# Sums of the Winograd products kept in PSUM, and the modulation units divided anew between VectorE and TensorE

## The chip, the cores and the metric

The kernel runs on one core of one Trainium2 chip. The metric is the device time of one execution in microseconds (us). The kernel before took 2699.28 us, the median of three runs (2695.43 to 2701.18).

## The reference, cut to what matters

Two layers are computed on 640 tokens (512 latent, 128 context) of 1024 dimensions. Each layer is a half-step SwiGLU FFN, a mixer of three head groups, and a second FFN half; after each of the three stands a LayerNorm. Each of the three is steered by a shift, a scale and a gate that come from a conditioning vector:

```python
mod = (silu(cond) @ w_mod[l] + b_mod[l]).reshape(9, 1024)      # for the latent and for the context tokens
h = x * (1 + mod[3 * slot + 1]) + mod[3 * slot]
f = (silu(h @ w1) * (h @ w3)) @ w2                             # FFN half, 1024 -> 2816 -> 1024
x = layernorm(alpha * x + 0.5 * mod[3 * slot + 2] * f)
```

All of it is in float32. A product is formed as three passes over operands that are split in a high and a low part (hi x hi, hi x lo, lo x hi).

## The kernel before, in words

**An FFN half.** The 2816 hidden columns are 22 tiles of 128, taken in the chunks 0-4, 4-7, 7-10, 10-14, 14-18 and 18-22. The first three tiles of a half are computed plainly; each of the other 19 is a `Pair`: the two weight tiles (w1 and w3) and the two halves of the tokens (320 columns each, LO and HI) are multiplied as a 2 x 2 block product by Winograd's form of Strassen's scheme, seven block products instead of eight. A block product is 12 matmuls of 320 columns. The chunks after the first hold 3, 3, 4, 4 and 4 pairs. After the pairs of a chunk come its rows: eight output tiles of `w2`, whose results VectorE adds to x (L610). `begun` starts the first two rows without the chunk's last hidden tile.

**Weights.** `Stream` (from L220) loads a pair's two tiles, GpSimd forms the sums s1 to s4 of their blocks (L259, four instructions for each pair), ScalarE rounds each block to its high part (L299, `wh`), and VectorE, or GpSimd for s2 and s4, forms the low part (L306, `wl`). There are six slots of each; a cast is issued five blocks ahead, so that it waits for the product before the one that is being issued to leave its slot.

**A pair, `Pair.run` from L898.** The products come in the order b11, b21, t4, t2, t3, t1, b22; P1 to P7 stand for them below. Each has a PSUM bank of its own (p1, p2, p6, p7, p3, and the two of a double bank p4 and p5). ScalarE copies p1 to SBUF (L895); VectorE forms the sums that Winograd's form wants, seven instructions that each add one bank to a tile in SBUF (L858, called from `c11`, `u2`'s lambda, `u3`, `u4` and `c12`). Then come SiLU of both halves on ScalarE (L863, L877), the gate products on VectorE (`gate1` L865, which calls the helper at L858, and `gate2` L881), the rounding `gh` on ScalarE (L886) and its low part `gl` on VectorE (L891).

**Order.** What follows a product is put in the list `later`, and `slot()` issues it after the next product's matmuls have been issued, so each engine's queue has it one product later; what such a function returns goes to the slot after that. The engines work through their queues in order. `mods(0)`, `mods(1)` and `mods(2)` stand after P2, P4 and P6 of a pair, and one call stands after each row.

**PSUM.** Four single banks (pool `pss`) serve p1, p2, p6, p7, p3 and others; a new tile takes the bank that was given back first.

**Modulation.** There are 144 units (layer, one of nine vectors, one of eight tiles of 128 columns), each 512 KB of `w_mod`. The first 24 are done on TensorE at the start. Of the other 120, some go to VectorE in an FFN half (`vec_mods`, L437: four SCALAR_TENSOR_TENSOR of 128 x 512 for each unit, L460, each with the read of its accumulator, and one small instruction, L463); `mods` issues (4 n + 4) / 95 of them at each call for n units, from the second chunk on. The others go to TensorE in a mixer (`mod_beside`, L411: 8 matmuls at L397 and one for the unit before, at L415). Such a unit is done beside each of the first `len(modq)` of 40 score units of the mixer, and ScalarE takes out the result (L422, L425). Before, 16 units go to VectorE in each of the first three halves, and 40 and 32 to TensorE in the two mixers.

Of the kernel before, what the change touches and what calls it, by code (L numbers as in the profile page):

```python
# [7 lines left out]
F32 = mybir.dt.float32  # L8
F32R = mybir.dt.float32r
BF16 = mybir.dt.bfloat16  # L10
AF = mybir.ActivationFunctionType
ALU = mybir.AluOpType
# [5 lines left out]
KD = D // P  # L18
T = 640
# [11 lines left out]
NC = 3  # L31
HN = T // 2
SLOTS = 6
BLOCKS = ("a11", "a12", "a22", "s2", "s3", "s1", "s4")
NEG = -1.0e30
CONST = (("cond", 16), ("bmod", 144), ("lng", 48), ("lnb", 48), ("sink", 16), ("subg", 2), ("gq", 4), ("sel", 2), 
         ("gkv", 256))
# [68 lines left out]
def trunk_kernel(tc, I, O):  # L106
    nc = tc.nc
    V, S, G, PE = nc.vector, nc.scalar, nc.gpsimd, nc.tensor
    from contextlib import ExitStack
    with ExitStack() as es:  # L110
# [10 lines left out]
        pe_ = pst = pool("e", 21)  # L121
# [6 lines left out]
        pm = pool("wm", 4)  # L128
# [7 lines left out]
        def u(p, n, dt=F32, cols=T, nm="u"):  # L136
            return p.tile([P, cols], dt, tag=nm, name=n)
# [3 lines left out]
        def uid():  # L141
            cnt[0] += 1
            return cnt[0]

        def bank(n="s"):
            return pss.tile([P, 512], F32, tag="s", name=f"{n}{uid()}")

        def dbl(n="d"):
            return psd.tile([P, 2, 512], F32, tag="d", name=f"{n}{uid()}")
# [173 lines left out]
        ws = Stream()  # L323
# [22 lines left out]
        def start(g):  # L346

            next(g)
            tasks.append(g)
# [8 lines left out]
        modq = []  # L358
# [76 lines left out]
        vecq = []  # L435
# [40 lines left out]
        def split(hi, lo, src):  # L476
            S.copy(hi, src)  # L477
            V.tensor_tensor(out=lo, in0=src, in1=hi.bitcast(F32), op=ALU.subtract)  # L478
# [334 lines left out]
        later = []  # L813

        def slot():

            cur, later[:] = later[:], []
            for fn in cur:
                nxt = fn()
                if nxt:  # L820
                    later.append(nxt)
# [8 lines left out]
        class Pair:  # L830


            def __init__(self, h, tb, last):
                self.last = last
                self.b11, self.b21, self.b22 = ([[a[:, c] for a in h[k]] for k in ks]
                                                for ks, c in ((range(4), slice(0, HN)), (range(4, 8), slice(0, HN)),
                                                              (range(4, 8), slice(HN, T))))
                self.t1, self.t2, self.t3, self.t4 = (Quarter(tb, i) for i in range(4))
                self.m, self.sl = u(pe_, f"pm{uid()}"), None

            def out(self):
                self.gh, self.gl = u(pe_, f"gh{uid()}", F32R), u(pe_, f"gl{uid()}", F32R)
                return self.gh, self.gl

            def mms(self, out, w, b, k):
                for i, (a, c) in enumerate(((0, 0), (0, 1), (1, 0))):
                    PE.matmul(out[:, :HN], w[a][:, k, :], b[k][c], start=k == 0 and i == 0, stop=k == 3 and i == 2)  # L847

            def prod(self, out, b, post=None, w=None):
                w = w or ws.get()  # L850
                for k in range(4):
                    self.mms(out, w, b, k)
                slot()
                if post:
                    later.append(post)

            def op(self, o, a, b, f):
                V.tensor_tensor(out=o, in0=a, in1=b[:, :HN], op=f)  # L858

            def c11(self, p2):  # L860
                self.sl = u(pe_, f"sl{uid()}")
                self.op(self.sl[:, LO], self.m[:, LO], p2, ALU.add)
                return lambda: S.activation(self.sl[:, LO], self.sl[:, LO], AF.Silu) and None  # L863

            def gate1(self):  # L865
                self.op(self.g[:, LO], self.g[:, LO], self.sl, ALU.mult)
                return self.half if self.last else None

            def half(self):
                split(self.gh[:, LO], self.gl[:, LO], self.g[:, LO])  # L870

            def c12(self, p3):
                self.op(self.sl[:, HI], self.m[:, LO], p3, ALU.add)
                return self.silu2

            def silu2(self):
                S.activation(self.sl[:, HI], self.sl[:, HI], AF.Silu)  # L877
                return self.gate2

            def gate2(self):  # L880
                V.tensor_tensor(out=self.g[:, HI], in0=self.g[:, HI], in1=self.sl[:, HI], op=ALU.mult)  # L881
                return self.hi

            def hi(self):
                c = HI if self.last else slice(0, T)
                S.copy(self.gh[:, c], self.g[:, c])  # L886
                return self.lo

            def lo(self):
                c = HI if self.last else slice(0, T)  # L890
                V.tensor_tensor(out=self.gl[:, c], in0=self.g[:, c], in1=self.gh[:, c].bitcast(F32), op=ALU.subtract)  # L891

            def start(self):
                p1, p2 = bank("p1"), bank("p2")
                self.prod(p1, self.b11, lambda: S.copy(self.m[:, LO], p1[:, :HN]) and None)  # L895
                self.prod(p2, self.b21, lambda: self.c11(p2))

            def run(self, mods, begun=False):  # L898
                m, op = self.m, self.op
                if not begun:  # L900
                    self.start()
                mods(0)
                p45 = dbl("p4")
                p4, p5 = p45[:, 0, :], p45[:, 1, :]
                self.prod(p4, self.t4)
                p6 = bank("p6")
                self.prod(p6, self.t2, lambda: op(m[:, LO], m[:, LO], p6, ALU.add))
                mods(1)
                p7 = bank("p7")

                def u3():
                    op(m[:, HI], m[:, LO], p7, ALU.add)
                    self.g = u(pe_, f"gf{uid()}")
                    op(self.g[:, LO], m[:, HI], p4, ALU.subtract)
                    return self.gate1
                self.prod(p7, self.t3, u3)

                def u4():
                    op(self.g[:, HI], m[:, HI], p5, ALU.add)
                    op(m[:, LO], m[:, LO], p5, ALU.add)  # L920
                self.prod(p5, self.t1, u4)
                mods(2)
                p3 = bank("p3")
                self.prod(p3, self.b22, lambda: self.c12(p3))

            def run_first(self, mods, other, ts):

                m, op = self.m, self.op
                self.start()
                mods(0)  # L930
                other.start()
                p3 = bank("p3")
                self.prod(p3, self.b22, None, ws.get(4))
                w22 = ws.get(0)
                p45, p6, p7 = dbl("p4"), bank("p6"), bank("p7")
                p4, p5 = p45[:, 0, :], p45[:, 1, :]
                wq = [ws.get(0), ws.get(0), ws.get(2), w22]
                for k in range(4):
                    for o, w, b in zip((p5, p7, p6, p4), wq, (self.t1, self.t3, self.t2, self.t4)):
                        self.mms(o, w, b, k)  # L940
                    mods(k)
                    next(ts, 0)
                slot()

                def post():
                    self.g = u(pe_, f"gf{uid()}")
                    op(m[:, LO], m[:, LO], p6, ALU.add)
                    op(m[:, HI], m[:, LO], p7, ALU.add)
                    op(self.g[:, LO], m[:, HI], p4, ALU.subtract)
                    op(self.g[:, HI], m[:, HI], p5, ALU.add)  # L950
                    op(m[:, LO], m[:, LO], p5, ALU.add)
                    later.append(self.gate1)
                    return self.c12(p3)
                later.append(post)

        LO, HI = slice(0, HN), slice(HN, T)

# [1089 lines left out]
        h = new_h()  # L2047
        first = [dbl("n"), dbl("n"), [bank("n"), bank("n")]]
# [23 lines left out]
        ts = tb_steps(tb, h)  # L2072
# [26 lines left out]
        for l in range(DEPTH):  # L2099
            if l:  # L2100
                tb, ts = tb_next
            h, first = ffn(l, 0, h, first, 0 if l else KD, 2 * KD, lambda a, n, b: rows_norm(a, n, l, 0, (l, 1), b),
                           alpha_first if l == 0 else lambda: alpha_x(l - 1, 2), tb, ts)
            modq += [vecq.pop(0) for _ in range((4 if l else 5) * KD)]
            h, first = mixer(l, h, first, lambda a, n, b: rows_norm(a, n, l, 1, (l, 2), b))
            nxt = (l + 1, 0) if l + 1 < DEPTH else None
            tb, ts = tb_next
            h, first = ffn(l, 1, h, first, 0, 0 if l else 2 * KD, lambda a, n, b: rows_norm(a, n, l, 2, nxt, b),
                           lambda: alpha_x(l, 1), tb, ts)


# [88 lines left out]
```

## Time and profile before

| what | value |
|---|---|
| median of three runs | 2699.28 us |
| the profiled execution | 2705.26 us, its span 2703.3 us |
| mean granted clock of TensorE | 0.976 |
| busy: TensorE, VectorE, ScalarE, GpSimd | 95%, 77%, 43%, 46% |

Times in the profile are microseconds from the start of the span. PE is TensorE, PEld its weight load, DVE VectorE, ACT ScalarE, POOL GpSimd, SP the queue that issues DMAs. A row `out<-in` names the tiles; L858 is line 858 of the kernel. PEclk is the clock that TensorE was granted, as a share of 2.4 GHz. Records of matmuls overlap, so that their mean duration is longer than the time from one to the next.

### The profile page before, as it was taken

What the parts mean: (1) busy time and instruction counts of PE and PEld (TensorE: products, weight loads), DVE (VectorE), ACT (ScalarE), POOL (GpSimd) and SP (SyncE); (2) the same over time, 40 slices, a digit from 0 to 9 for tenths busy, and PEclk for the clock granted to TensorE, in tenths of its full rate; (3) what the DMA queues carried; (4) which work ended last, traced back from release to release, by engine and by line L of the source; (5) the groups of instructions that cost most, each with busy time, mean ns of one, the idle gap of its engine ahead of it and who ended that gap; (6) DMA issues with size and microseconds to landing.
All of it is one profiled execution on the core that took longest, in us unless ns stands there. A gap on an engine that the chain in (4) does not pass through costs nothing. (4 is left out here: it accounts for less than half of the span.)

```text
span 2703.3 us, 49877 instructions
## 1 busy us (share of the span) xinstructions
PE 2555.0 (95%) x18662; PEld 2453.0 (91%) x18662; DVE 2072.3 (77%) x3759; ACT 1175.9 (43%) x2596; POOL 1244.0 (46%) x973
## 2 busy tenths in 40 slices
PE   7999999899999999999989999998998999999997
PEld 6999999888778999999989999998887798999997
DVE  6599889856764879988987998898476558777776
ACT  5233333545575533333353333334545745334333
POOL 2345445522444554544555454454233456435545
PEclk9999999999999999999989999998999999999998
DMA  7333332354344223333222333323543331222222
GB/s 273 116 98 101 111 97 83 117 152 136 91 130 156 71 96 100 103 101 109 68 83 84 112 103 101 110 87 108 158 134 98 103 114 40 82 82 87 79 86 71
DMA packets 130545, 285.89 MB, mean 106 GB/s; under 512 B 16832, under 2 KB 34560, under 8 KB 129664
## 3 DMA queue, kind: packets, MB, share of 16 engines
q1 hardware_dynamic: 130304, 282.70, 33.2%
q8 instruction: 148, 2.42, 0.4%
q14 instruction: 93, 0.76, 0.1%
HBM read 254.95 MB, written 8.81 MB: 98 GB/s over the span
## 5 line engine op out<-in xcount | busy, mean ns | idle before, releaser
L306 DVE TENSOR_TENSOR wl<-wr,wh 128x512 fp32r<-128x512 f32 (+1 forms) x524 | 518.3, 1003 | 74.1 <-ACT wh L299 72.5
L299 ACT CAST wh<-wr 128x512 fp32r<-128x512 f32 (+1 forms) x570 | 333.3, 607 | 479.4 <-DMA wr<-in_w 296.9
L485 PE MATMUL o<-gh,wh 128*128 128x256 f32 (+1 forms) x1408 | 439.5, 312 | 19.4 <-ACT gh L886 11.7
L485 PE MATMUL o<-gl,wh 128*128 128x256 f32 (+1 forms) x1408 | 439.0, 312 | 1.8 <-DVE gl L478 0.3
L485 PE MATMUL o<-gh,wl 128*128 128x256 f32 (+1 forms) x1408 | 436.7, 310 | 0.0
L847 PE MATMUL p<-hh,wh 128*128 128x320 f32 x1216 | 378.4, 311 | 16.8 <-DVE pm L858 16.8
L847 PE MATMUL p<-hl,wh 128*128 128x320 f32 x1216 | 378.2, 311 | 6.2 <-DVE hl L1010 6.2
L847 PE MATMUL p<-hh,wl 128*128 128x320 f32 x1216 | 378.1, 311 | 0.0
L259 POOL TENSOR_TENSOR ws<-wr 128x512 f32<-128x512 f32 x76 | 111.5, 1468 | 545.8 <-DMA wr<-in_w 482.8
L299 ACT CAST wh<-ws 128x512 fp32r<-128x512 f32 x304 | 185.9, 621 | 361.6 <-PE p L847 153.4
L306 POOL TENSOR_TENSOR wl<-ws,wh 128x512 fp32r<-128x512 f32 x152 | 241.3, 1591 | 193.6 <-ACT wh L299 193.1
L610 DVE SCALAR_TENSOR_TENSOR x<-o,gat,x 128x128 f32<-128x128 f32 (+2 forms) x404 | 192.9, 524 | 139.6 <-PE o L485 136.6
L485 PEld LDWEIGHTS o<-gh,wh 128*128 128x128 f32 x1408 | 267.8, 190 | 23.0 <-ACT gh L886 14.5
L485 PEld LDWEIGHTS o<-gl,wh 128*128 128x128 f32 x1408 | 268.1, 190 | 6.7 <-DVE gl L891 4.8
L485 PEld LDWEIGHTS o<-gh,wl 128*128 128x128 f32 x1408 | 267.9, 190 | 0.0
L847 PEld LDWEIGHTS p<-hh,wh 128*128 128x128 f32 x1216 | 229.9, 189 | 19.0 <-issue 18.9
L847 PEld LDWEIGHTS p<-hl,wh 128*128 128x128 f32 x1216 | 230.0, 189 | 7.4 <-DVE hl L1010 7.4
L847 PEld LDWEIGHTS p<-hh,wl 128*128 128x128 f32 x1216 | 230.0, 189 | 0.3 <-DVE wl L306 0.3
L460 DVE SCALAR_TENSOR_TENSOR scr<-wv,cb 128x512 f32<-128x512 f32 x192 | 181.2, 944 | 0.0
L259 POOL TENSOR_TENSOR ws<-wr,wr 128x512 f32<-128x512 f32 x76 | 130.2, 1713 | 0.0
L259 POOL TENSOR_TENSOR ws<-wr,ws 128x512 f32<-128x512 f32 x76 | 129.9, 1709 | 0.0
L259 POOL TENSOR_TENSOR ws<-ws,wr 128x512 f32<-128x512 f32 x76 | 119.1, 1567 | 6.0
(434 smaller groups left out, 6633.9 us busy)
## 6 DMA issues: line engine op xcount, KB each, us to landing
wr<-in_w SPq DMA_DIRECT2D x176, 512.0 KB, 4.2
wm<-in_wmod SPq DMA_DIRECT2D x192, 256.0 KB, 3.9
wr<-in_w SPq DMA_DIRECT2D x128, 256.0 KB, 2.7
wv<-in_wmt SPq DMA_DIRECT2D x96, 256.0 KB, 4.0
wr<-in_w SPq DMA_DIRECT2D x64, 192.0 KB, 2.4
wr<-in_wint SPq DMA_DIRECT2D x24, 512.0 KB, 4.2
wr<-in_wo SPq DMA_DIRECT2D x16, 512.0 KB, 3.8
xd<-x SPq DMA_DIRECT2D x16, 320.0 KB, 5.1
```

The costliest lines, as they stand in the source:

```text
L259: G.tensor_tensor(out=o, in0=x0, in1=x1, op=op)
L299: S.copy(hl[0], src[:, c0:c1])
L306: eng.tensor_tensor(out=t2, in0=src, in1=t.bitcast(F32), op=ALU.subtract)
L460: V.scalar_tensor_tensor(out=scr, in0=w[2 * i + hf], scalar=1.0, in1=cb[:, 2 * st + hf, :], op0=ALU.mult, op1=ALU.mult, accum_out=a[:, 2 * ...
L485: PE.matmul(out[:, :cn], whl[a][:, k, :], b[:, c0:c0 + cn], start=k == 0 and i == 0, stop=k == n - 1 and i == 2)
L610: V.scalar_tensor_tensor(out=c, in0=src, scalar=gat[:, d, s:s + 1], in1=c, op0=ALU.mult, op1=ALU.add)
L847: PE.matmul(out[:, :HN], w[a][:, k, :], b[k][c], start=k == 0 and i == 0, stop=k == 3 and i == 2)
```

## The change: what it does

Within a pair, products that are only added to each other go into one bank: p1, then t2's product, then t3's are accumulated in `px`, and t1's product and b22's in `pz`. Between two of them ScalarE copies the sum so far to SBUF (to `sl` or to `g`). The order of the products becomes b11, b21, t4, t2, t1, t3, b22, and the order of the weight blocks follows it. VectorE keeps four of the seven additions, ScalarE makes four copies instead of one, a pair takes four single banks and no double one, and the two gate products become one of 640 columns but in the last pair of a chunk.

In each of the first three FFN halves VectorE gets 24 units instead of 16, and the mixers get 24 and 24 instead of 40 and 32. `run_first`, which nothing calls, goes.

```diff
-BLOCKS = ("a11", "a12", "a22", "s2", "s3", "s1", "s4")
+BLOCKS = ("a11", "a12", "a22", "s2", "s1", "s3", "s4")
...
-            def prod(self, out, b, post=None, w=None):
-                w = w or ws.get()
+            def prod(self, out, b, post, more=False):
+
+                w = ws.get()
                 for k in range(4):
-                    self.mms(out, w, b, k)
+                    for i, (a, c) in enumerate(((0, 0), (0, 1), (1, 0))):
+                        PE.matmul(out[:, :HN], w[a][:, k, :], b[k][c], start=not more and k == 0 and i == 0, stop=k == 3 and i == 2,
+                                  skip_group_check=more)
                 slot()
-                if post:
-                    later.append(post)
+                later.append(post)
+
+            def add(self, o, ps, f=ALU.add):
+                V.tensor_tensor(out=o, in0=ps[:, :HN], in1=o, op=f)
+
+            def gate(self, c):
+                V.tensor_tensor(out=self.g[:, c], in0=self.g[:, c], in1=self.sl[:, c], op=ALU.mult)
+
+            def split(self, c, nxt=None):
+
                 S.copy(self.gh[:, c], self.g[:, c])
+
+                def lo():
+                    V.tensor_tensor(out=self.gl[:, c], in0=self.g[:, c], in1=self.gh[:, c].bitcast(F32), op=ALU.subtract)
+                    return nxt
+                return lo
+
+            def run(self, mods):
+
+                sl = self.sl = u(pe_, f"sl{uid()}")
+                px, py = bank("px"), bank("py")
+                self.prod(px, self.b11, lambda: S.copy(sl[:, LO], px[:, :HN]) and None)
+
+                def c11():
+                    self.add(sl[:, LO], py)
+                    return lambda: S.activation(sl[:, LO], sl[:, LO], AF.Silu) and None
+                self.prod(py, self.b21, c11)
                 mods(0)
+                pw = bank("pw")
+
+                def c4():
+                    self.g = u(pe_, f"gf{uid()}")
+                    S.copy(self.g[:, LO], pw[:, :HN])
+                self.prod(pw, self.t4, c4)
+                self.prod(px, self.t2, lambda: S.copy(sl[:, HI], px[:, :HN]) and None, True)
                 mods(1)
+                pz = bank("pz")
+                self.prod(pz, self.t1, lambda: S.copy(self.g[:, HI], pz[:, :HN]) and None)
+
+                def c2():
+                    self.add(self.g[:, LO], px, ALU.subtract)
+                    self.add(self.g[:, HI], px)
+                    if self.last:
+                        self.gate(LO)
+                        return lambda: self.split(LO)
+                self.prod(px, self.t3, c2, True)
                 mods(2)
+
+                def c12():
+                    self.add(sl[:, HI], pz)
+                    return silu
+
+                def silu():
+                    S.activation(sl[:, HI], sl[:, HI], AF.Silu)
+                    return gate
+
+                def gate():
+                    c = HI if self.last else slice(0, T)
+                    self.gate(c)
+                    return lambda: self.split(c)
+                self.prod(pz, self.b22, c12, True)
...
-            h, first = ffn(l, 0, h, first, 0 if l else KD, 2 * KD, lambda a, n, b: rows_norm(a, n, l, 0, (l, 1), b),
+            h, first = ffn(l, 0, h, first, 0 if l else KD, 3 * KD, lambda a, n, b: rows_norm(a, n, l, 0, (l, 1), b),
...
-            modq += [vecq.pop(0) for _ in range((4 if l else 5) * KD)]
+            modq += [vecq.pop(0) for _ in range(3 * KD)]
...
-            h, first = ffn(l, 1, h, first, 0, 0 if l else 2 * KD, lambda a, n, b: rows_norm(a, n, l, 2, nxt, b),
+            h, first = ffn(l, 1, h, first, 0, 0 if l else 3 * KD, lambda a, n, b: rows_norm(a, n, l, 2, nxt, b),
```

Of the old code the helpers `op`, `c11`, `gate1`, `half`, `c12`, `silu2`, `gate2`, `hi`, `lo`, `start` and the old `run` go; they stand in the listing above.

## Rows read from the trace of the kernel before

**Rows 1.** The page, part 1: TensorE, busy us and share.
```profile
PE 2555.0 (95%) x18662; PEld 2453.0 (91%) x18662; DVE 2072.3 (77%) x3759; ACT 1175.9 (43%) x2596; POOL 1244.0 (46%) x973
```
**Rows 2.** Windows of the four halves: length, PE, PEld, DVE, ACT, POOL, PEclk, DMA.
```profile
134.14:470.21 336.07, 326.09 (x2187) 323.25 (x2187) 302.88 (x505) 122.78 (x230) 167.93 (x103) 0.99 0.31 98
999.23:1336.72 337.49, 327.12 (x2187) 323.66 (x2187) 305.23 (x508) 123.75 (x231) 167.46 (x103) 0.99 0.31 97
1474.59:1807.68 333.09, 324.71 (x2187) 322.08 (x2187) 303.41 (x505) 123.17 (x230) 165.97 (x103) 0.99 0.31 99
2331.43:2651.66 320.23, 320.23 (x2187) 320.23 (x2187) 240.38 (x373) 125.93 (x232) 156.09 (x103) 1.00 0.26 81
```
**Rows 3.** Windows of chunks of four pairs and of their rows, second and last half.
```profile
1202.45:1254.19 51.74, 49.94 (x339) 49.45 (x339) 49.83 (x74) 21.38 (x40) 30.85 (x19) 1.00 0.29 93
1254.19:1283.56 29.37, 28.48 (x192) 28.02 (x192) 22.58 (x45) 7.30 (x13) 7.75 (x5) 1.00 0.40 129
...
2524.84:2574.28 49.44, 49.44 (x339) 49.44 (x339) 41.92 (x59) 22.79 (x42) 29.61 (x19) 1.00 0.23 70
2574.28:2602.39 28.11, 28.11 (x194) 28.11 (x194) 14.54 (x28) 6.62 (x13) 6.83 (x5) 1.00 0.33 104
```
**Rows 4.** Waits: who waited for whom, us in total, times, longest.
```profile
PE p L847 <- DVE pm L858: 16.8, 8, 3.5
...
PE o L485 <- ACT gh L886: 11.7, 13, 1.1
```
**Rows 5.** Timeline of PE, P2 of a chunk's fourth pair: start, us, what it waited for.
```profile
1243.39 0.39 PE L847 MATMUL p<-hh,wh 128*128 128x320 f32 x1 [1.80 <-DVE pm L858]
```
**Rows 6.** Timeline of DVE, second and third pair of that chunk.
```profile
1222.29 0.47 DVE L858 TENSOR_TENSOR sl<-pm,p 128x320 f32<-128x320 f32 x1
...
1225.71 1.92 DVE L891 TENSOR_TENSOR gl<-gf,gh 128x640 fp32r<-128x640 f32 x1
...
1236.53 1.57 DVE L881 TENSOR_TENSOR gf<-gf,sl 128x320 f32<-128x320 f32 x1
1238.02 0.47 DVE L858 TENSOR_TENSOR sl<-pm,p 128x320 f32<-128x320 f32 x1
```
**Rows 7.** Timeline of DVE, third pair of the last half's chunk.
```profile
2553.65 0.47 DVE L858 TENSOR_TENSOR sl<-pm,p 128x320 f32<-128x320 f32 x1
```
**Rows 8.** Groups by line: busy us, mean ns of one, idle time before.
```profile
L460 DVE SCALAR_TENSOR_TENSOR scr<-wv,cb 128x512 f32<-128x512 f32 x192 | 181.2, 944 | 0.0
...
L895 ACT COPY pm<-p 128x320 f32<-128x320 f32 x76 | 31.2, 410 | 0.0
L460 DVE DVE_READ_ACCUMULATOR scr<-wv,cb 128x1 f32 x192 | 15.2, 79 | 0.0
```
**Rows 9.** Tile scr and line 858: ns shortest/median/longest, first and last start.
```profile
L460 DVE SCALAR_TENSOR_TENSOR scr<-wv,cb x192: 675/683/1830, 131.8 to 1814.7; 128x512 f32<-128x512 f32 x192
...
L858 DVE TENSOR_TENSOR pm<-pm,p x228: 472/475/489, 97.9 to 2651.7; 128x320 f32<-128x320 f32 x114
```
**Rows 10.** Timeline of ACT behind the late sum of the second pair.
```profile
1222.40 0.73 ACT L886 CAST gh<-gf 128x640 fp32r<-128x640 f32 x1 [1.63 <-DVE gf L881]
1223.04 0.46 ACT L863 ACTIVATE sl<-sl 128x320 f32<-128x320 f32 x1
1223.41 0.60 ACT L299 CAST wh<-wr 128x512 fp32r<-128x512 f32 x1
```
**Rows 11.** Window at a lowered clock, just behind a wait of PE.
```profile
1325.20:1328.60 3.40, 3.40 (x15) 3.40 (x14) 3.30 (x10) 0.00 (x0) 0.00 (x0) 0.51 0.30 87
```
**Rows 12.** Timeline of PE, a modulation unit in the first mixer.
```profile
844.44 0.28 PE L415 MATMUL t<-const,ms 128*128 128x2 f32 x2
844.65 0.64 PE L397 MATMUL t<-wm,silc 128*32 128x128 f32 x16
845.23 0.44 PE L1133 MATMUL tr<-idn,ep 128*128 128x128 f32 x2
```
**Rows 13.** Window of the first mixer's last 16 score units.
```profile
789.48:844.33 54.85, 51.93 (x628) 43.49 (x627) 25.31 (x73) 35.41 (x120) 18.36 (x30) 1.00 0.48 150
```

More of the change, by code (lines that the diff above doesn't have):

```diff
@@ L838, in __init__ @@
                 self.t1, self.t2, self.t3, self.t4 = (Quarter(tb, i) for i in range(4))
-                self.m, self.sl = u(pe_, f"pm{uid()}"), None
             def out(self):
@@ L843, in out @@
                 return self.gh, self.gl
-            def mms(self, out, w, b, k):
-                for i, (a, c) in enumerate(((0, 0), (0, 1), (1, 0))):
-                    PE.matmul(out[:, :HN], w[a][:, k, :], b[k][c], start=k == 0 and i == 0, stop=k == 3 and i == 2)
-            def prod(self, out, b, post=None, w=None):
-                w = w or ws.get()
+            def prod(self, out, b, post, more=False):
+                w = ws.get()
                 for k in range(4):
-                    self.mms(out, w, b, k)
+                    for i, (a, c) in enumerate(((0, 0), (0, 1), (1, 0))):
+                        PE.matmul(out[:, :HN], w[a][:, k, :], b[k][c], start=not more and k == 0 and i == 0, stop=k == 3 and i == 2,
+                                  skip_group_check=more)
@@ L853, in prod @@
                 slot()
-                if post:
-                    later.append(post)
[L857 to L882, printed above, removed]
@@ L884, in hi @@
-            def hi(self):
-                c = HI if self.last else slice(0, T)
-                S.copy(self.gh[:, c], self.g[:, c])
[L887 to L901, printed above, removed]
-                mods(0)
[L903 to L907, printed above, removed]
-                mods(1)
[L909 to L921, printed above, removed]
-                mods(2)
-                p3 = bank("p3")
-                self.prod(p3, self.b22, lambda: self.c12(p3))
@@ L926, in run_first @@
[L926 to L954, printed above, removed]
```

## The prediction

> **What bounds the kernel now.** The page first: TensorE is busy 95% of the span, so what counts is what TensorE executes and what it waits for [rows 1]. Then the windows of the four FFN halves, each from the first product of its second chunk to the last product: the three halves in which VectorE also computes modulation units take 336.07, 337.49 and 333.09 us, the last one, which has none, 320.23 us, and there TensorE never rests [rows 2]. The same matmuls cost 46.0 us more in three halves. The column DVE tells why: about 303 us against 240. One chunk shows where: four pairs take 51.74 us instead of 49.44, their rows 29.37 instead of 28.11 [rows 3]. With 1.26 us for each of 15 row parts (12 lie inside the windows) the rows hold 15 of the 46.0 us, the pairs 31. The waits name them: in the pairs TensorE waits for VectorE's additions (8 times, 16.8 us), in the rows for the rounded gate product (13 times, 11.7 us) [rows 4]. One such wait is 1.80 us, in a fourth pair [rows 5].
>
> VectorE is late there, and by how much is seen from the addition that forms the first half of the SiLU's input (c11, `sl<-pm,p`). A pair of TensorE takes 49.44 / 4 = 12.36 us, a product 1.77. In the last half c11 starts 4.1 us after its pair's P1 (2553.65, the third pair, which starts at 2524.84 + 24.7) [rows 7]. With modulation it starts 7.5 us after P1 in the second pair and 10.8 in the third [rows 6]. From one to the next VectorE needs 15.73 us for a pair that TensorE does in 12.36. The kernel before bears this: P2 of the fourth pair waits only for an addition of the third pair's fifth slot, so VectorE may be some 7 us late, and in the chunk's last pair it catches up, since GpSimd has no sums to form.
>
> **The change, part by part.**
>
> *Additions and gates in a pair.* Three additions of 0.47 us go; their starts follow each other by 0.40, so VectorE gets 1.2 us. Two gate products, 1.57 us each beside a working GpSimd, become one of 640 columns, which I price as the low part of the same size, 1.92: another 1.2 [rows 6].
>
> *More modulation in the halves.* (4 x 24 + 4) / 95 = 1.05 instructions for each call of `mods` instead of 0.72; three calls make 1.0 more in each pair. One takes 0.94 us in the mean, and 0.08 for its accumulator: 1.0 us [rows 8]. The ends are 0.68 and 1.83 [rows 9]. I take the mean, whose rows lie in these same stages.
>
> Together a pair costs VectorE 15.73 - 1.2 - 1.2 + 1.0 = 14.3 us: still 2.0 above TensorE's 12.36. The other end comes from the last half, 41.92 / 4 = 10.5 us for a pair [rows 3], less 1.2, plus 3.16 instructions at their shortest, 0.68 + 0.08: 11.7, which TensorE would never feel. I take the 2.0, because its rows come from a chunk in the state in question.
>
> The rows show what lies between the two. An instruction that reads two tiles in SBUF takes 0.68 us or up to 1.83, an addition that reads a bank 0.472 to 0.489, whatever GpSimd does [rows 9]. The Trainium skill says so in "SBUF — State Buffer", section "Who interferes with whom": a VectorE instruction with two SBUF inputs contends with a GpSimd instruction that reads SBUF, one with at most one SBUF input does not. By that rule the change gives back three instructions that never waited and adds one that does. Were every added one blocked, the sum would be higher (the last rival); by the mean row it is the sum below.
>
> *What TensorE now waits for.* A bank that is added to may not be written before ScalarE has copied the sum so far: P6 (t3) waits for the copy that follows P4, P7 for the one that follows P5. The pass between is one product, 1.77 us. Behind c11 ScalarE still has, in its queue's order, the SiLU, the copy of P3, a cast and then that copy: with starts 0.37, 0.38, 0.51 and 0.41 us apart [rows 8, 10], and c11's own 0.47 and some 0.15 of signals, 2.3 us. P6 begins 8.83 us after P1, so c11 must start by 6.5. VectorE may now be 2.4 us late instead of 7. What is queued behind: the rounding of the gate product stands before the SiLU and waits 1.63 us for VectorE already now [rows 10]. So an excess of 2.0 a pair turns into a wait before P6 in every pair but the one that uses up the slack. I take three pairs' excess in a chunk of four and two in a chunk of three, less 0.8 of slack: 6.0 - 0.8 and 4.0 - 0.8. Per half 3 x 5.2 + 2 x 3.2 = 22; three halves 66 us where the pairs paid 31. So **+35**.
>
> *The rows.* VectorE is held closer to TensorE, and in a chunk's last pair the second addition of `sl` comes directly after P7 and a short queue. The waits before the rows go: 15 x 1.26 = **-19**.
>
> *The clock.* Behind a wait like that of [rows 5] the granted clock falls to 0.51, its lower level of 1.2 GHz, for 3.4 us in one case [rows 11], 1.7 us lost each time; the three halves lie at 0.99 [rows 2], two such periods each. With some seven waits of about 2 us in a half instead of three I take three periods more: 9 x 1.7 = **+15**; between none and 30.
>
> *The last half.* VectorE needs 42 us for 49 and loses work. Only in a chunk's last pair, where the cast before the copy waits for its DMA, I expect 0.5 us: **+1.5**.
>
> *The mixers.* 24 units leave TensorE. One takes 0.79 us there, from 844.44 to 845.23 [rows 12]. The stretch that loses 16 of them has TensorE busy 51.93 of 54.85 us [rows 13]. The ends are 19 and nothing, if the score units' other steps set the pace; as TensorE has 95%, I take 0.5 of each: **-12**. Their loads move to the halves, where DMA engines are a third busy [rows 2]; nothing. ScalarE's three more copies are 3 x 0.41 us in a pair; ScalarE is busy 22 us of 49 [rows 3, 8]: nothing but their place in the queue, counted above. The freed double bank and the fourth single one: a new tile takes the bank given back first, which is py's, then pw's; px's is needed only for P3 of the next pair. Nothing.
>
> Sum: 35 - 19 + 15 + 1.5 - 12 = +20.5. On the profiled execution's 2705.26 that makes 2725.8; the median of the three runs lies 6.0 below it, so I predict **2720 us**.
>
> **The rivals.**
>
> *VectorE keeps up (faster).* If c11 starts by 6.5 us after P1 in all pairs, the new waits don't arise. It hangs on the excess e of a pair. The terms above are 39 e - 12 for the pairs (nine chunks of 3 e - 0.8, six of 2 e - 0.8), 7.5 e for the clock, and -31 - 19 + 1.5 - 12 for the rest; they cross zero at e = 1.56, a pair of 13.9 us. With e = 1 the change gives 26 us, 2673; with none 60 (the clock's and the pairs' terms at 0, and no less), about 2638. For it speaks the other end of the price, 11.7 us; against it the 15.73 of the chunk that was looked at. Chance 0.28.
>
> *One gives what the other takes (no change).* With e between 1.45 and 1.68 the new waits cost what the rows and the mixers give, within 5 us. Chance 0.12.
>
> *Every added instruction meets GpSimd (much slower).* At 1.83 instead of 1.02 for the 54 additional ones in pairs, 44 us more: about 2764. Against it: the median is 0.68. Chance 0.10. That the banks do not do what is meant, an addition being done twice or a bank reread late, would show as waits at every P6, in the last half too: 76 pairs x 0.7 us, the same size, and is counted here.
>
> **How the numbers follow.** The forecast has 0.50, between 2705 and 2755: an excess from 1.7 to 2.7 us makes that. The range reaches down past the nearer form of the faster rival, to 2668, and up to the slow one, 2762. About 0.2% (5.4 us) is what a measurement can tell from no change. Slower: 0.50 + 0.10 = 0.60; same 0.12; faster 0.28.
>
> **What would show it.** Right: waits of PE for an ACT copy at the third product into `px`, c11 at 6 to 9 us after P1 in second and later pairs, chunks of four pairs at 54 to 56 us in the first three halves, rows at 28.1, the last half as before. Wrong: chunks of four at 51 us or less, or a first mixer shorter by 15 us. The steps that I trust least are the 2.0 us of excess and the clock.

## The result, and the profile after

The changed kernel takes 2721.26 us, the median of four runs (2719.54 to 2723.33), against 2697.36 us of the kernel before in four (2694.57 to 2701.18): a ratio of 1.0094 with a 95% interval from 1.0077 to 1.011. 23.9 us were lost.

The page's first part stands beside [rows 1]: TensorE has 18.4 us less to do, and its share falls from 95% to 93%.

```profile
PE 2536.6 (93%) x18230; PEld 2426.9 (89%) x18230; DVE 2069.6 (76%) x3693; ACT 1243.0 (46%) x2778; POOL 1246.2 (46%) x973
```

The windows show where it was lost: first the four halves, cut as in [rows 2]; then the sums over the 15 pair parts of the first three halves and over the 12 row parts between them; then one chunk of four and its rows, and the same in the last half, as in [rows 3].

```profile
139.13:484.03 344.90, 327.14 (x2187) 320.29 (x2187) 309.90 (x512) 142.44 (x287) 167.01 (x103) 1.00 0.34 108
1000.37:1347.90 347.53, 327.88 (x2187) 321.81 (x2187) 309.05 (x512) 142.13 (x287) 167.28 (x103) 1.00 0.33 107
1481.62:1829.13 347.51, 328.23 (x2187) 321.81 (x2187) 310.67 (x512) 141.88 (x286) 166.92 (x103) 1.00 0.34 108
2343.41:2665.99 322.58, 321.42 (x2187) 320.27 (x2187) 225.91 (x307) 143.03 (x287) 156.36 (x103) 1.00 0.25 81
...
sum 746.79, PE 690.10 PEld 670.76 DVE 705.78 ACT 365.70 POOL 442.28; mean PE 46.01 PEld 44.72 DVE 47.05 ACT 24.38 POOL 29.49
...
sum 293.15, PE 293.15 PEld 293.15 DVE 223.84 ACT 60.76 POOL 58.93; mean PE 24.43 PEld 24.43 DVE 18.65 ACT 5.06 POOL 4.91
...
1211.32:1265.74 54.42, 50.76 (x339) 49.45 (x339) 51.94 (x75) 26.62 (x54) 30.93 (x19) 1.00 0.35 115
1265.74:1293.69 27.95, 27.95 (x194) 27.95 (x192) 19.86 (x44) 6.08 (x12) 6.75 (x5) 1.00 0.28 91
2537.93:2588.01 50.08, 49.70 (x339) 49.44 (x339) 38.80 (x45) 26.94 (x55) 29.86 (x19) 1.00 0.24 74
```

The same two sums of the kernel before, pairs and rows:

```profile
sum 693.47, PE 675.83 PEld 673.38 DVE 663.97 ACT 286.61 POOL 420.40; mean PE 45.06 PEld 44.89 DVE 44.26 ACT 19.11 POOL 28.03
...
sum 313.18, PE 302.09 PEld 295.62 DVE 247.55 ACT 83.08 POOL 80.95; mean PE 25.17 PEld 24.63 DVE 20.63 ACT 6.92 POOL 6.75
```

The pairs of the three halves are 53.3 us longer, their rows 20.0 us shorter (TensorE never rests in them now). The last half is 2.35 us longer, the start, up to the first window, 139.13 instead of 134.14, 5.0 us. Between the windows, where the mixers lie, the changed kernel is shorter: by 12.7 (516.34 instead of 529.02), 4.2 (no mixer) and 9.5 us. Together 53.3 - 20.0 + 2.35 + 5.0 - 26.3 = +14.3, which is, to 0.1 us, the difference of the two spans (2717.7 and 2703.3). The rest of the 23.9 lies in which executions were profiled: that of before was 7.9 us above its median, that of after 1.7 below. How much single executions scatter is seen in the stretch with the second mixer: it takes from 509.6 to 523.9 us in the kernels below that have 24 units in it.

Who waited for whom, on TensorE (us in total, times, longest):

```profile
PE px L849 <- ACT sl L886: 41.8, 35, 2.1
...
PE pz L849 <- ACT gf L889: 7.6, 8, 1.5
...
PE pw L849 <- DVE gf L855: 5.1, 4, 1.7
PE pw L849 <- DVE mod L389: 4.8, 1, 4.8
```

The wait for VectorE's additions has fallen from the 16.8 us of [rows 4] to 5.1, the wait for `gh` before the rows is gone; in their place stands the third product into `px` (P6), which waits for ScalarE's copy of the bank. Two examples from the timeline, of one chunk of four. First PE, P6 of the second, third and fourth pair:

```profile
1232.96 0.41 PE L849 MATMUL px<-tvb,wh 128*128 128x320 f32 x1 [0.36 <-ACT sl L886]
...
1246.78 0.42 PE L849 MATMUL px<-tvb,wh 128*128 128x320 f32 x1 [0.73 <-ACT sl L886]
...
1261.95 0.41 PE L849 MATMUL px<-tvb,wh 128*128 128x320 f32 x1 [2.10 <-ACT sl L886]
```

Then ScalarE before the first of these waits, and before the last:

```profile
1230.65 0.73 ACT L862 CAST gh<-gf 128x640 fp32r<-128x640 f32 x1 [1.01 <-DVE gf L858]
1231.29 0.47 ACT L877 ACTIVATE sl<-sl 128x320 f32<-128x320 f32 x1
1231.66 0.40 ACT L884 COPY gf<-pw 128x320 f32<-128x320 f32 x1
1231.96 0.61 ACT L299 CAST wh<-wr 128x512 fp32r<-128x512 f32 x1
1232.48 0.42 ACT L886 COPY sl<-px 128x320 f32<-128x320 f32 x1
...
1255.24 0.47 ACT L905 ACTIVATE sl<-sl 128x320 f32<-128x320 f32 x1 [2.35 <-DVE sl L855]
1255.61 0.41 ACT L873 COPY sl<-px 128x320 f32<-128x320 f32 x1
1255.92 1.14 ACT L299 CAST wh<-wr 128x512 fp32r<-128x512 f32 x2
...
1260.96 0.62 ACT L299 CAST wh<-wr 128x512 fp32r<-128x512 f32 x1 [2.36 <-DMA wr<-in_w]
1261.48 0.42 ACT L886 COPY sl<-px 128x320 f32<-128x320 f32 x1
```

In the second pair the copy stands behind the rounding, the SiLU and the rest of the queue, which waited for VectorE. In the last pair it stands behind a weight cast that waits 2.36 us for its load. That is a second chain, and a dearer one: within the three halves the P6 of the last pairs wait 26 us in the 15 chunks, all the other P6 14.

### The profile page after: what moved, and what is told of

Read it like the earlier page. It is cut to its first block, busy times and chain, and to the rows that moved or that the text cites. A ratio compares the mean times of both kernels' runs of the same rounds, so it can differ in the third digit from the quotient of the medians.

```text
span 2717.7 us, 48714 instructions
## 1 busy us (share of the span) xinstructions
PE 2536.6 (93%) x18230; PEld 2426.9 (89%) x18230; DVE 2069.6 (76%) x3693; ACT 1243.0 (46%) x2778; POOL 1246.2 (46%) x973
## 3 DMA queue, kind: packets, MB, share of 16 engines
q8 instruction: 144, 2.36, 0.4%
## 5 line engine op out<-in xcount | busy, mean ns | idle before, releaser
L306 DVE TENSOR_TENSOR wl<-wr,wh 128x512 fp32r<-128x512 f32 (+1 forms) x524 | 528.0, 1024 | 88.7 <-ACT wh L299 84.9
L460 DVE SCALAR_TENSOR_TENSOR scr<-wv,cb 128x512 f32<-128x512 f32 x288 | 269.9, 937 | 0.1
L306 DVE TENSOR_TENSOR wl<-ws,wh 128x512 fp32r<-128x512 f32 x152 | 142.8, 952 | 0.6
L849 PE MATMUL px<-hh,wh 128*128 128x320 f32 x456 | 141.6, 311 | 0.0
L849 PE MATMUL px<-hh,wl 128*128 128x320 f32 x456 | 141.5, 310 | 0.0
L849 PE MATMUL px<-hl,wh 128*128 128x320 f32 x456 | 141.4, 310 | 0.0
L849 PE MATMUL pz<-hh,wh 128*128 128x320 f32 x380 | 119.4, 314 | 7.6 <-ACT gf L889 7.6
L849 PE MATMUL pz<-hl,wh 128*128 128x320 f32 x380 | 118.2, 311 | 0.0
```

The source lines that it names most:

```text
L306: eng.tensor_tensor(out=t2, in0=src, in1=t.bitcast(F32), op=ALU.subtract)
L460: V.scalar_tensor_tensor(out=scr, in0=w[2 * i + hf], scalar=1.0, in1=cb[:, 2 * st + hf, :], op0=ALU.mult, op1=ALU.mult, accum_out=a[:, 2 * ...
L849: PE.matmul(out[:, :HN], w[a][:, k, :], b[k][c], start=not more and k == 0 and i == 0, stop=k == 3 and i == 2, skip_group_check=more)
```

## The experiments

The kernel before ran beside each of three groups of runs: 2694.58 us in the first, 2696.78 in the second, 2693.57 in the third. Each ratio is to the one beside it.

**One half of the change at a time.** The sums in PSUM with the old division of the units:

```diff
-            h, first = ffn(l, 0, h, first, 0 if l else KD, 3 * KD, ...
+            h, first = ffn(l, 0, h, first, 0 if l else KD, 2 * KD, ...
...
-            modq += [vecq.pop(0) for _ in range(3 * KD)]
+            modq += [vecq.pop(0) for _ in range((4 if l else 5) * KD)]
...
-            h, first = ffn(l, 1, h, first, 0, 0 if l else 3 * KD, ...
+            h, first = ffn(l, 1, h, first, 0, 0 if l else 2 * KD, ...
```

> The accumulation in PSUM with the old division of the modulation units (16 in each of the first three halves, 40 and 32 in the mixers). Theory A (the loss is VectorE's excess in a pair, made into a wait before P6): a pair has 1.0 us of modulation less, so the excess falls from about 2.0 to 1.0; chunks of four about 51.6 us instead of 54 to 59, the three halves about 9 us shorter each than in the changed kernel, the mixers 14 us longer in all: 2699 to 2712 us. Rival B (the accumulation itself costs, whatever VectorE has to do): halves of 345 us stay and the mixers' 14 us come on top: 2730 us or more.

Measured: 2700.41 us, a ratio of 1.002 (1.0002 to 1.0038). The other half alone is the old pair with these three lines as the change has them:

> The old pair with its own bank for each product, and the new division of the units (24 in each of the first three halves, 24 in each mixer). Theory A: the excess of a pair grows by 1.0 us to about 4.4; 3 us more in each chunk of four, 1 in each of three, rows longer too; halves of about 347 us, mixers 14 us shorter: 2710 to 2722 us. Rival B (only the accumulation costs): the halves stay at 333 to 337 us and the mixers give 14 us: about 2684 us.

Measured: 2714.84 us, 1.0068 (1.0048 to 1.0089). Theory A's times hold in both, B's in neither. Not all of A's steps do: with the sums alone the chunks of four take 53.3 us in the mean, not 51.6. The two halves of the change cost 5.8 and 20.3 us, together 26.1, about what the whole does: **the units cost the time, the sums in PSUM hardly any.** The sums of the windows, pairs and rows of the first three halves, show how each comes about; with the sums in PSUM alone:

```profile
sum 713.74, PE 684.99 PEld 675.30 DVE 652.82 ACT 361.06 POOL 419.86; mean PE 45.67 PEld 45.02 DVE 43.52 ACT 24.07 POOL 27.99
...
sum 293.11, PE 293.11 PEld 293.11 DVE 213.64 ACT 66.13 POOL 80.64; mean PE 24.43 PEld 24.43 DVE 17.80 ACT 5.51 POOL 6.72
```

With the units alone:

```profile
sum 722.03, PE 686.91 PEld 679.31 DVE 698.41 ACT 291.45 POOL 442.43; mean PE 45.79 PEld 45.29 DVE 46.56 ACT 19.43 POOL 29.50
...
sum 317.98, PE 305.87 PEld 298.35 DVE 262.35 ACT 77.47 POOL 60.52; mean PE 25.49 PEld 24.86 DVE 21.86 ACT 6.46 POOL 5.04
```

The sums give 20.1 us back in the rows and take 20.3 in the pairs. The units take 28.6 in the old pairs and 4.8 in their rows; on top of the sums they take 33.1 in the pairs and nothing in the rows (293.15 instead of 293.11). In both cases that is more than the stretches with the mixers give back, 23.6 and 12.4 us.

**The place of the copy in ScalarE's queue.** Four kernels move it. In the first the SiLU and the rounding go behind the copy, and t4's product, P3, goes to the double bank (the expectations call it the fourth product):

```diff
-                    return lambda: S.activation(sl[:, LO], sl[:, LO], AF.Silu) and None
...
-                pw = bank("pw")
+                pw = dbl("pw")[:, 0, :]
...
-                self.prod(px, self.t2, lambda: S.copy(sl[:, HI], px[:, :HN]) and None, True)
+                def c5():
+                    S.copy(sl[:, HI], px[:, :HN])
+                    S.activation(sl[:, LO], sl[:, LO], AF.Silu)
+                    return held.pop()() if held else None
+                self.prod(px, self.t2, c5, True)
...
-                    return lambda: self.split(c)
+                    if self.last:
+                        return lambda: self.split(c)
+                    held.append(lambda: self.split(c))
```

> The changed kernel, with the copy of px after t2 ahead of the SiLU and of the rounding in ScalarE's queue (those two go one product later), and the fourth product in the double bank instead of a single one. Theory A (P6 waits only because that copy stands behind work that waits for VectorE): no wait of PE px for ACT is over 0.3 us, c11 may start 9 us and more after P1, chunks of four 51 to 53 us, and the first pair of the first half loses its wait of 4.8 us: about 2690 to 2705 us. Rival C (VectorE is short over the whole half, and the wait only moves): the waits come back before the rows (o for gh) or at P7, the halves stay at 342 us or more: 2708 us or more.

Measured: 2721.52 us, 1.0094 (1.0069 to 1.0118): theory A's expectation failed. C's time holds, though not the places it named: the waits are split over P4 and P6 and are no smaller:

```profile
PE px L849 <- ACT sl L887: 36.2, 24, 2.2
PE px L849 <- ACT sl L873: 20.8, 24, 1.7
```

L887 is the copy that P6 waits for; P6 of every last pair still waits 1.2 to 2.2 us for it, behind the cast that waits for its load. L873 is the copy of the first product: with VectorE later, it stands behind the second SiLU of the pair before, and now P4 waits. Next, that one copy directly behind its product, ahead of the cast:

```diff
-                later.append(post)
+                if now:
+                    post()
+                else:
+                    later.append(post)
...
-                self.prod(px, self.t2, lambda: S.copy(sl[:, HI], px[:, :HN]) and None, True)
+                self.prod(px, self.t2, lambda: S.copy(sl[:, HI], px[:, :HN]) and None, True, True)
```

> The changed kernel, with one instruction moved: the copy of px after t2 stands directly behind its product, ahead of the weight cast that was before it in ScalarE's queue. In the changed kernel the P6 of the last pair of each of the 15 chunks waits 26 us in all, and in one looked at ScalarE stood 2.36 us in that cast, whose load came late. Theory D (the load's lateness passes through the cast to the copy and to P6): these waits fall under 0.3 us, the halves get 6 to 9 us shorter each: 2695 to 2706 us. Theory A alone (VectorE's excess is paid somewhere in any case): the waits move to P4, P7, to the next products' weights or to the rows, the halves stay within 3 us: 2712 us or more.

Measured: 2712.11 us, 1.007 (1.0046 to 1.0093). The P6 of the last pairs of the three halves no longer wait at all, so the cast was what they waited behind, as D says. But P7, which waits for the copy of `pz`, now waits more (7.6 us in the changed kernel):

```profile
PE pz L849 <- ACT gf L892: 37.7, 28, 2.5
```

A is right that the time is paid elsewhere: the halves take 343.4, 348.1 and 346.8 us, within 1.5 us of the changed kernel's. The 2712 lies at A's bound. With all four copies so, the first SiLU and the rounding one product later, and the double bank:

> The changed kernel with all four copies directly behind their products, the first SiLU and the rounding one product later, and the fourth product in the double bank, so that no copy stands behind work that waits for VectorE or for a load. Theory A+D: no wait of PE for a copy (px for ACT sl, pz for ACT gf) is over 0.3 us, and VectorE may be 8 us and more late; the first half's first pair loses 4.8 us: halves of 326 to 335 us, 2670 to 2695 us. Rival C (VectorE's work in the halves is too much whatever the queues): the same microseconds come back as waits before the rows or for a weight's low part, halves of 340 us or more: 2708 us or more.

Measured: 2720.65 us, 1.008 (1.0049 to 1.0112): A+D failed, C's time holds, though the waits stand at P7 and not where it put them:

```profile
PE pz L849 <- ACT gf L892: 45.5, 17, 3.7
```

ScalarE before one of these waits, of 3.43 us, which ended at 1254.74:

```profile
1252.77 0.62 ACT L299 CAST wh<-wr 128x512 fp32r<-128x512 f32 x1 [3.53 <-DMA wr<-in_w]
1253.29 0.72 ACT L865 CAST gh<-gf 128x640 fp32r<-128x640 f32 x1
1253.92 0.46 ACT L880 ACTIVATE sl<-sl 128x320 f32<-128x320 f32 x1
1254.29 0.40 ACT L892 COPY gf<-pz 128x320 f32<-128x320 f32 x1
```

It is the cast again, still waiting for its load, one copy further on. The pairs' waits come to 53 us, hardly less than the 56.7 of the changed kernel, but they are fewer and longer, and TensorE is at half speed for 43.8 us in the three halves instead of 6.8. The window at that wait shows it:

```profile
1253.20:1260.00 6.80, 5.26 (x21) 5.26 (x22) 5.37 (x12) 3.56 (x9) 0.00 (x0) 0.50 0.43 130
```

Each of the twelve waits of 2.6 to 3.7 us at P7 has a stretch at half speed beside it (3.4 us, twice 6.8), the three of 1.6 to 1.7 us have none. The same queues with the old division:

> The same queues as in the run with direct copies, with the old division of the units (16 in each of the first three halves, 40 and 32 in the mixers). Theory A+D: with an excess of about 1.0 a pair VectorE is never 8 us late, halves of 321 to 326 us, mixers as before: 2660 to 2685 us, faster than the kernel before. Rival C: halves of 333 us or more as in the run with the sums alone: 2692 us or more.

Measured: 2687.33 us, 0.9967 (0.995 to 0.9984), between the two theories' ranges and **faster than the kernel before**, by 0.3%. The halves, 332.5 to 333.6 us, are C's and not A+D's; the waits of P7 are 24.9 us instead of 45.5. With 16 units in a half the direct copies, and what goes with them (double bank, later SiLU and rounding), turn the 5.8 us lost with the sums alone into 9.5 won; with 24 they bring nothing. What they bring hangs on how late VectorE is.

**The double bank alone.**

> The changed kernel with the fourth product in the double bank and nothing else. Theory E (in the first pair of the first half P3 waits 4.8 us because its bank was last held by a product of a modulation unit, and four pairs wait 5.1 us in all for VectorE to read the bank of the pair before): both waits go, the first pair is 5 us shorter, the rest within 3 us: 2711 to 2717 us. Rival F (P3 waits for data, as TensorE does in the other halves' first pairs): no change, 2718 to 2724 us.

Measured: 2723.04 us, 1.0096 (1.008 to 1.0112). In the changed kernel's first pair P3 waits for a modulation product to be read:

```profile
96.43 0.61 PE L849 MATMUL pw<-tvb,wh 128*128 128x320 f32 x1 [4.80 <-DVE mod L389]
```

This wait falls to 0.69 us, as E says, and the four waits for VectorE's reading go too. But P6 of the same pair now waits 1.8 us, so that the first window begins at 136.76 instead of 139.13, 2.4 us earlier and not 5, and nothing of it arrives at the end: the waits for `sl` L886 grow from 41.8 to 51.6 us. The time is F's, though F's reason is not the one.

**Less of it in the pairs.** The same units, fewer at each call in the pairs and more in the rows:

```diff
-                    credit[0] += (4 * nvec + 4) / 95 * (1 if when is None else 1)
+                    credit[0] += (4 * nvec + 4) / 95 * (1.53 if when is None else 0.6)
```

> The changed kernel, with 0.6 instead of 1 share of the modulation instructions at each call in the pairs and 1.53 at each call in the rows (the number of units is the same). Theory A: a pair has 1.26 instructions less, 1.2 to 1.5 us, the excess falls to 0.5 to 0.8: chunks of four 50.5 to 52 us, rows still 28 to 28.5, halves of 328 to 333: 2672 to 2695 us. Rival C (VectorE is short over the whole half): rows of four grow to 30 us and more and the time stays over 2708 us.

Measured: 2707.15 us, 1.0046 (1.0029 to 1.0062), between the two. The pairs of the three halves take 730.74 us instead of 746.79, their rows 295.48 instead of 293.15: C's long rows did not come, but VectorE comes late out of the rows (c11 of a first pair 8.7 to 10.8 us after P1 behind rows of three), and the last P6 of the chunks of four still wait 1.5 to 2.2 us.

**The load behind the cast.** In the last pair the late load is that of a `w2` tile. There are two buffers for raw tiles; one is free once VectorE has formed the low part. Four kernels give the first four of these low parts to GpSimd:

```diff
                         src, m, n = self.raw[r], shape[1], shape[0] * shape[1]
+                        if any(isinstance(j[1], str) for j in self.jobs[max(len(self.w) - 4, 0):len(self.w)]):
+                            eng = G
```

> The changed kernel, with the low parts of the first four w2 tiles behind a chunk's pairs formed by GpSimd, which has no sums to form in the last pair, instead of VectorE. Theory D (VectorE's lateness in the last pair keeps the raw buffer of a w2 tile, so the next load, its cast and the copy behind it are late): the P6 waits of the last pairs (26 us in 15 chunks) fall under 0.5 us each, chunks of four to 51 to 53 us: 2692 to 2706 us. Rival A alone (VectorE's excess over the whole chunk is paid whatever the loads do): waits of the same size elsewhere in the pairs, 2713 us or more.

Measured: 2724.19 us, 1.0106 (1.0085 to 1.0127): D failed in this form. The last pair shows why; ScalarE, GpSimd and the DMA queue:

```profile
1260.08 0.47 ACT L907 ACTIVATE sl<-sl 128x320 f32<-128x320 f32 x1 [2.36 <-DVE sl L857]
1260.45 0.41 ACT L875 COPY sl<-px 128x320 f32<-128x320 f32 x1
1260.76 1.14 ACT L301 CAST wh<-wr 128x512 fp32r<-128x512 f32 x2
...
1265.87 0.62 ACT L301 CAST wh<-wr 128x512 fp32r<-128x512 f32 x1 [2.43 <-DMA wr<-in_w]
...
1261.46 3.39 POOL L308 TENSOR_TENSOR wl<-wr,wh 128x512 fp32r<-128x512 f32 x2 [2.37 <-ACT wh L301]
...
1263.17 2.03 SPq L243 DMA_DIRECT2D wr<-in_w  x2
```

The chain begins before the cast: the SiLU waits 2.36 us for VectorE's last addition of the pair before, and the cast of the first `w2` tile stands behind it. GpSimd is free, but waits for that cast too, and then needs 1.7 us for a low part where VectorE needed 0.67. So the load starts at 1263.17, 2.4 us after the cast began, as in the changed kernel (at 1258.17, 2.3 us after 1255.92), and the next cast waits as long.

> The same with the new division of the units (24 in each of the first three halves, 24 in each mixer). Theory D: the P7 waits of the last pairs (45.5 us, 17 times) go, and the mixers' 14 us are kept: halves of 322 to 330 us, 2655 to 2690 us. Rival A alone: the waits move to the first pairs or to the rows, halves of 338 us or more, 2705 us or more.

Measured: 2701.25 us, 1.0028 (1.0009 to 1.0047): neither range, 19 us less than without GpSimd's part (16 when each is compared with the kernel before beside it).

> Direct copies, the fourth product in the double bank, the old division of the units, and the low parts of the first four w2 tiles behind a chunk's pairs on GpSimd. Theory D: the P7 waits of the last pairs in the run without the last of these (24.9 us, 15 times) go, halves of 321 to 324 us: 2660 to 2672 us. Rival A alone: 2682 us or more.

Measured: **2676.21 us, 0.9938 (0.9918 to 0.9957)**, faster than both kernels and 11 us less than without GpSimd's part (8 by the runs beside them), though not in D's range. Pairs and rows:

```profile
sum 694.38, PE 673.71 PEld 670.03 DVE 634.67 ACT 348.89 POOL 497.58; mean PE 44.91 PEld 44.67 DVE 42.31 ACT 23.26 POOL 33.17
...
sum 293.13, PE 293.13 PEld 293.13 DVE 218.42 ACT 76.58 POOL 80.48; mean PE 24.43 PEld 24.43 DVE 18.20 ACT 6.38 POOL 6.71
```

The pairs cost what they cost before (693.47), the rows 20 us less. The waits for the copy of `pz`, which D says go, are 20.6 us, 14 times, nearly all in last pairs (24.9 without GpSimd's part).

> The kernel before, with only the low parts of the first four w2 tiles behind a chunk's pairs on GpSimd. Theory D does not bear on it, since no product there waits for a copy. If VectorE's lateness at a chunk's end is what its waits come from (P2 of the fourth pair 16.8 us, rows 11.7 us), part of it goes, most of the rows': 2680 to 2692 us. If the excess is built up in the pairs before, the P2 waits stay and the rows gain a few us: 2688 to 2697 us.

Measured: 2712.49 us, 1.0071 (1.0045 to 1.0097), slower than either branch said. P2 of the fourth pairs still waits (14.0 us, 8 times), and the rows grow from 313.18 to 325.28 us. The waits for `gh` before the rows are 15.4 us instead of 11.7; why is not shown. In these four kernels moving the low parts paid in the two with direct copies and cost or brought nothing in the other two; that the place of the copies is the reason is not shown.

## Why the prediction was right, and where its steps were not

The forecast was 2720 us, slower, and the measured 2721.26 lies on it. The mechanism that it named is there: VectorE's excess becomes a wait of P6 for ScalarE's copy. But of the 40 us that P6 waits in the three halves only 14 come by the queue that it described; 26 are those of the last pairs. And that the number fits so closely is luck. Between the two profiled executions, from which the sum of +20.5 was worked out, the difference is +14.3, and the terms missed in opposite directions: the pairs +56.7 instead of +35, the clock -5.1 instead of +15, the stretches between the windows -26.3 instead of -12, the start +5.0 instead of nothing.

*The excess of a pair.* VectorE's pace is read from the four additions c11 of the chunk that starts at 1211.32:

```profile
1216.12 0.48 DVE L855 TENSOR_TENSOR sl<-py,sl 128x320 f32<-128x320 f32 x1
...
1230.54 0.48 DVE L855 TENSOR_TENSOR sl<-py,sl 128x320 f32<-128x320 f32 x1
...
1244.36 0.48 DVE L855 TENSOR_TENSOR sl<-py,sl 128x320 f32<-128x320 f32 x1
...
1257.08 0.47 DVE L855 TENSOR_TENSOR sl<-py,sl 128x320 f32<-128x320 f32 x1
```

From the first pair to the second, before any P6 has waited, it is 14.4 us, where 14.3 was worked out: an excess of 2.06. Then it falls, to 13.8 and in the last pair to 12.7. In the changed kernel an instruction of the units takes 937 ns in the mean, from 675 to 1808, and an addition from a bank 473 to 492, whatever GpSimd does, as in [rows 8, 9]; the rule of the Trainium skill that was named beside them ("SBUF — State Buffer", section "Who interferes with whom") agrees with both. In second and later pairs c11 starts 4.7 to 8.2 us after P1; the forecast said 6 to 9. Chunks of four take 53.9 to 59.4 us, in the mean 55.7; it said 54 to 56. The longest are the first ones of four, where VectorE comes 8.3 to 8.5 us late out of the rows of three; that was not foreseen.

*Pairs and clock, 35 + 15.* Measured in the pairs: 53.3 together, but +56.7 without the clock and -3.4 by it. **The clock was the wrong step**, "three periods more" in each half. In the windows of the three halves five periods of 3.4 us at half speed (two of them in one stretch, at a wait of 3.5 us) became two: four in the pairs became two, and one in a row part went. One wait of 2.15 us (P6 at 1178.06) has such a period behind it, another, shown above (2.10 at 1261.95), has none:

```profile
1179.20:1182.60 3.40, 3.40 (x14) 3.40 (x14) 1.98 (x4) 1.80 (x4) 0.00 (x0) 0.50 0.54 154
1262.00:1265.40 3.40, 3.40 (x23) 3.40 (x24) 2.98 (x8) 1.11 (x3) 0.00 (x0) 1.00 0.58 172
```

Of the eight waits of 2.0 to 2.2 us in the changed kernel's pairs two have one, of the shorter ones none. The kernel before could have told it: of its seven waits of 1.7 to 2.0 us there two have one, and the wait of [rows 5], from which the forecast priced "each time", has none, as the clock of 1.00 of its chunk in [rows 3] shows. With the sums alone all five waits of 1.9 to 2.1 us have one; what decides is not shown.

The 35 also rests on two figures that do not hold. The pairs of before paid 25.9 us in the windows and their rows 20.0, not 31 and 15: one row part was taken for all. And the 0.8 us of slack in each chunk, 12 us in all, has no row behind it.

*The last pair of a chunk.* The prediction took **"0.5 us" for the cast that waits for its DMA, and in the last half alone.** In the last half it is 0.35 us, in each chunk of four, and +2.35 for the half instead of +1.5. In the other three it was the largest single item: 26 us, and 21 even with the sums alone. By the prediction's own terms the sums alone, with an excess of 1.0, would have changed the pairs by 27 - 31 = -4 us; they took 20.3 more. The other P6 waits, which the prediction had at 5.2 and 3.2 us for each chunk, came to 14 us in all: the excess of 2.06 holds for one step of a chunk of four, not for three.

*Part of a wait is counted as work.* In the chunk at 1211.32 the five waits come to 3.65 us, the chunk is 4.98 longer than in [rows 3]'s 49.44, and TensorE's busy time grew by the missing 1.32: 0.26 us for each wait. At that price the some 65 waits in the pairs of the three halves carry 17 us (an estimate), and the two periods at half speed 3.4; so 56.7 us of idle time there cost 79 over the clean 667.6 (9 x 49.44 + 6 x 37.11), all but 2 us accounted for.

*Rows, -19.* Measured -20.0 in the 12 parts within the windows, for which the forecast had -15; 1.7 of it are the clock's. *Mixers, -12.* The stretches between the windows give 26.3 in these two executions, of which 4.2 lie where there is no mixer; with the scatter of 14 us named above this does not contradict it, and no more can be said. *Banks, "nothing".* Wrong by the 4.8 us of the first pair, where the bank given back first was one that a modulation product had held, and by the 5.1 us of P3's four waits for VectorE's reading; the double bank, which takes both away, did not make the kernel faster. The forecast looked at the pairs in their steady state and not at the first.

*The rivals.* That VectorE keeps up is refuted by the 14.4 us; its pair of 11.7 had every added instruction at its shortest. That the banks do not do what is meant is refuted by the last half, where P6 waits in four of its 19 pairs only, 0.5 us at most.

What stays open: which link of the last pair's chain is the one to cut. Moving the low part did not do it, and neither did moving the copies alone; a third buffer for raw tiles was not tried.

## What to carry to other kernels

When a result stays in a bank that is added to, the copy between two sums becomes work that the matmuls wait for, and everything ahead of it in its engine's queue comes with it: a SiLU that waits for another engine, a cast that waits for a load. Follow the queue of the engine that makes the copy in the first and last round of a loop too, not only in the middle. Putting the copy directly behind its product paid here with 16 units on VectorE in a half (2687 us instead of 2700) and not with 24 (2721 both times), so look first how late the engine is that the rest of the queue waits for. Work that is moved to an engine that is already late can cost more there than it gives back where it came from: the 24 units that moved took 33 us in the three halves of the old pair, and the whole kernel lost 20.

## What the runs showed of the hardware that was not expected

A wait of TensorE costs more than the idle time that the trace shows: 0.26 us for each of the five waits of the chunk at 1211.32, in its busy time; why is not shown. And the granted clock does not follow the total of the waits: with direct copies and 24 units, where twelve waits are 2.6 to 3.7 us long, it stood at half speed for 43.8 us within the three halves, in the changed kernel, whose waits come to 57 us instead of 53 but to at most 2.15 each, for 6.8.
